# One set of rooms for the moving pieces of attention and feed-forward, filled across the change between them

## The chip, the cores and the metric

The kernel runs on one core of a Trainium2 chip, as one launch. The metric is the device time of the launch in microseconds (us). The kernel before was timed three times: 3040.87, 3048.89 and 3052.48 us, median 3048.89 us. The execution of the profile took 3045.82 us; the span of its trace, from the first to the last instruction, is 3044.1 us. A change of 0.5% is about 15 us.

## What is computed

One inference step of one decoder layer, in float32, for a prompt of 2048 new rows and, with the same weights, for 8 samples of 4 new rows each (32 rows). The model width is 1024.

```python
def decoder_layer(x, s_gla, s_ssm, conv_buf, mk, mv, lw):
    m, s_gla, s_ssm, conv_buf = mixer(rmsnorm(x, lw['ln_mix_pre']), s_gla, s_ssm, conv_buf, lw)
    h = x + rmsnorm(m, lw['ln_mix_post'])
    a = cross_attend(rmsnorm(h, lw['ln_xa_pre']), mk, mv, lw['w_xq'], lw['w_xo'])
    h = h + rmsnorm(a, lw['ln_xa_post'])
    hf = rmsnorm(h, lw['ln_ffn_pre'])
    f = (jax.nn.silu(hf @ lw['w_gate']) * (hf @ lw['w_up'])) @ lw['w_down']
    h = h + rmsnorm(f, lw['ln_ffn_post'])
    return h, s_gla, s_ssm, conv_buf
```

`mixer` is one product with `w_in`, then gated linear attention (GLA) and a state-space part (SSD) with a causal convolution over four rows (`full[:, j:j + t] * lw['ssd_conv_w'][j]`), and a product with `w_out`. For the samples the mixer starts from given states (`state_gla`, `state_ssm`, `state_conv`), and cross attention reads a cache of keys and values for each sample. `w_gate` and `w_up` are 1024 x 2816, `w_down` is 2816 x 1024.

## The kernel before, in words

**Products.** TensorE (PE) multiplies in a reduced float32 form. To keep float32 precision each operand is split into a high part, written by ScalarE (ACT), and a low part, the rest, written by VectorE (DVE); each product is three matmuls (lines 127 to 129). The large products of the second part of the program use in addition a scheme of Strassen's kind: two 2 x 2 block matrices are multiplied with seven products of blocks instead of eight. One operand is *stationary* (loaded into PE as weights) and is made for each unit of work, in tiles named `s`, from an input tile `raw` and sums of it (class `Unit`: the high part in line 1502, the low part in line 1504, the sums in line 1484). The other operand is *moving* and is kept for a whole pass: seven **pieces**, each with a high and a low part, kept in seven **rooms** (tiles `r0` to `r6`).

**Passes.** The second part of the program, from about 918 us on, is a row of passes: "o" (mixer output projection), "s" (attention scores), "v" (attention values), each of 8 units of 256 prompt rows; then three feed-forward passes "g" (gate and up; of 22 units each, over blocks of 768, 768 and 512 prompt rows, the last with the samples); then four passes "d" (down). A unit is seven **groups** of matmuls, one group for each product of blocks, in the order `TURN = [0, 1, 3, 2, 5, 4, 6]`. A group is 12 matmuls, with 512 moving columns in "o", "s" and "v" and 384 in the first two "g" passes. The last group of a unit stands behind the first group of the next one; at the change from "v" to "g" it stands ahead of it. Groups accumulate into PSUM tiles `accA` (two of them), `accB` and `accC`, which ACT and DVE evacuate.

**Filling the rooms.** Class `Pieces` loads each piece in two halves from DRAM into a staging tile `st` (three buffers, which the post-processing also uses) by a DMA of the SP queue; `larger` writes the high part (ACT, line 1566), `smaller` writes the low part (DVE, line 1570) and then loads a later half. For "v" and "g" a half is 512 KB, or 256 KB for the smaller half of a "g" piece. A piece may go into a room when the piece that is in it has had its last matmul. In general the loop over groups makes one half after each group of the last unit of a pass and after each group of the first unit of the next one. The change from "v" to "g" is an exception: rooms of "o", "s" and "v" have `RW = 2048` columns for the high and for the low part, those of "g" have 1536, and `change_rooms` closes the one pool (`rx`) and opens the other (`rf`). So no half is made in the last "v" unit. Behind its last group `change_rooms` is called and two halves are made, and from there on two halves are made after each group of the first "g" unit. For this pass two halves are loaded ahead, for the others three.

**Order of issue.** The groups, the pieces, the evacuations and the post-processing (`posts`: generators, one step after each group; for "v" they are residual, norm, transposes on PE in line 1686, and the writing of the seven feed-forward operands `xp` to DRAM from the POOL queue) are issued in the order in which the loop calls them, and `pin` fixes that order on each engine. Two more queues of generators are stepped at the rates in `RATES` (tenths of a step per group): `aux` (sums of weight blocks) and `back` (the samples' whole layer up to the feed-forward). Steps of `back` are not pinned; a scheduler places their instructions near the group in which they are made. `back` starts in the first "g" pass, when the last of the posts of "v" is done.

**The samples' mixer** (`sample_mixer`) is the first generator of `back`. In one step it makes masks (`rsel`, `rmk` on POOL in lines 931 to 935; `blk`, `bm`, `rst` and others on DVE), loads the convolution rows `cvo`, convolves (lines 984 and 986: 8 and 24 DVE instructions) and applies SiLU; `sample_ssd` and `sample_gla` follow in small steps. In each of them a loop over the 8 samples loads a state, updates it and stores it (for SSD lines 1097 to 1107: two buffers `Ms`, multiplied on POOL in line 1104, added on DVE in line 1105, stored from the POOL queue).

## Time and profile before

| what | value |
|---|---|
| median of the three runs | 3048.89 us |
| profiled execution, its own time | 3045.82 us |
| its span | 3044.1 us |
| PE busy | 2884.3 us (95% of the span) |
| DVE busy | 2087.5 us (69%) |
| ACT busy | 1525.7 us (50%) |
| POOL busy | 544.3 us (18%) |
| mean granted clock of PE | 0.977 |

The time inside the device beside the span is 1.7 us. PE is busy nearly everywhere, so the places where it is not are what can be saved: the profile shows for each instruction how long its engine was idle before it and what ended that idle time ("[2.56 <-ACT r L1566]": 2.56 us, ended by the ACT instruction of line 1566 that wrote `r`). "Busy" of PE counts a matmul as long as it lasts, so a lower clock shows as longer matmuls and not as idle time; the column PEclk, the clock that was granted, has to be read beside it. The change from "v" to "g" lies at about 1469 us.

### The profile page before, as it was taken

How to read it: one execution, taken by the hardware profiler on the slowest of the kernel's cores; microseconds unless marked ns; L12 is line 12 of the kernel's file. 1: busy time of each engine (PE TensorE's matmuls, PEld its weight loads, DVE VectorE, ACT ScalarE, POOL GpSimd, SP SyncE). 2: the span in 40 equal slices, each digit the busy share in tenths (PEclk: the TensorE clock that was granted, in tenths of full speed). 3: DMA queues.
4: the chain of work that ended last, by engine and by line, in shares of the span. 5: the costliest groups of instructions: out<-in, count | busy, mean ns of one | idle time of the engine just before them, and what ended most of it. 6: DMA issues, size and time to landing. Idle time of an engine off the chain costs nothing.

```text
span 3044.1 us, 42288 instructions
## 1 busy us (share of the span) xinstructions
PE 2884.3 (95%) x15207; PEld 2408.6 (79%) x15207; DVE 2087.5 (69%) x3915; ACT 1525.7 (50%) x3044; POOL 544.3 (18%) x749
## 2 busy tenths in 40 slices
PE   8999999999997999999689999999999998999997
PEld 8887777787775778877588888888999995587875
DVE  7666676666737677677587777776678884566576
ACT  4454443554445677776554434433455553444453
POOL 2142341121321321024222100010000000011122
PEclk9999999999999999999799999999999999999998
DMA  7345543242256676467646455774243345767788
GB/s 239 118 152 161 169 125 118 70 128 75 78 187 226 242 263 227 153 202 237 195 177 212 163 172 186 258 265 160 101 150 121 119 141 183 245 139 192 158 210 246
DMA packets 154769, 529.89 MB, mean 174 GB/s; under 512 B 19360, under 2 KB 22608, under 8 KB 143040
## 3 DMA queue, kind: packets, MB, share of 16 engines
q1 hardware_dynamic: 93168, 331.75, 34.1%
q0 software_dynamic: 49152, 170.46, 18.4%
q10 hardware_dynamic: 12240, 24.99, 2.5%
q8 instruction: 120, 1.97, 0.3%
q14 instruction: 89, 0.73, 0.1%
HBM read 373.04 MB, written 154.09 MB: 173 GB/s over the span
## 4 chain that ended last, share of the span: by engine, by line
PE 57%; issue 16%; DMA 7%; DVE 6%; ACT 5%; POOL 2%; POOLq 0%; DVEq 0%; ACTq 0%; SPq 0%
PE accA L127 7%; PE accA L128 7%; PE accA L129 7%; PE accC L127 4%; PE acc L127 4%; PE acc L128 4%; PE acc L129 4%; PE accC L128 4%; PE accC L129 4%; PE accB L127 2%; PE accB L128 2%; PE accB L129 2%; PE mx L1911 1%; PE mx L1686 1%; DMA st<-wT 1%
## 5 line engine op out<-in xcount | busy, mean ns | idle before, releaser
L127 PE MATMUL accA<-r,s 128*128 128x512 f32 (+2 forms) x1792 | 645.3, 360 | 39.0 <-ACT r L1566 13.4
L129 PE MATMUL accA<-r,s 128*128 128x512 f32 (+2 forms) x1792 | 633.6, 354 | 7.1 <-DVE s L1504 6.2
L128 PE MATMUL accA<-r,s 128*128 128x512 f32 (+2 forms) x1792 | 633.9, 354 | 6.7 <-DVE r L1570 6.6
L127 PEld LDWEIGHTS accA<-r,s 128*128 128x128 f32 x1792 | 341.7, 191 | 114.7 <-ACT r L1566 17.5
L1502 ACT ACTIVATE s<-sum 128x512 fp32r<-128x512 f32 (+2 forms) x488 | 289.3, 593 | 268.4 <-DVE sum L1484 102.7
L128 PEld LDWEIGHTS accA<-r,s 128*128 128x128 f32 x1792 | 342.3, 191 | 40.8 <-DVE r L1570 12.0
L129 PEld LDWEIGHTS accA<-r,s 128*128 128x128 f32 x1792 | 341.9, 191 | 38.7 <-DVE s L1504 9.0
L127 PE MATMUL accC<-r,s 128*128 128x512 f32 (+2 forms) x896 | 325.3, 363 | 17.1 <-ACT r L1566 6.8
L1504 DVE TENSOR_TENSOR s<-sum,s 128x512 fp32r<-128x512 f32 (+2 forms) x488 | 308.8, 641 | 35.2 <-ACT s L1502 31.9
L129 PE MATMUL accC<-r,s 128*128 128x512 f32 (+2 forms) x896 | 317.9, 355 | 7.0 <-DVE s L1504 7.0
L128 PE MATMUL accC<-r,s 128*128 128x512 f32 (+2 forms) x896 | 317.6, 354 | 1.0 <-DVE r L1570 0.9
L1504 DVE TENSOR_TENSOR s<-raw,s 128x512 fp32r<-128x512 f32 (+2 forms) x366 | 234.3, 640 | 59.1 <-ACT s L1502 57.6
L1502 ACT ACTIVATE s<-raw 128x512 fp32r<-128x512 f32 (+2 forms) x366 | 218.2, 596 | 54.1 <-PE accC L129 51.3
L121 ACT ACTIVATE whi<-wraw 128x1024 fp32r<-128x1024 f32 (+2 forms) x148 | 137.1, 941 | 211.3 <-PE acc L128 107.2
L127 PEld LDWEIGHTS accC<-r,s 128*128 128x128 f32 x896 | 172.0, 192 | 61.4 <-issue 10.2
L122 DVE TENSOR_TENSOR wlo<-wraw,whi 128x1024 fp32r<-128x1024 f32 (+2 forms) x148 | 166.8, 1136 | 63.4 <-ACT whi L121 62.7
L129 PEld LDWEIGHTS accC<-r,s 128*128 128x128 f32 x896 | 171.8, 192 | 24.7 <-DVE s L1504 8.7
L1570 DVE TENSOR_TENSOR r<-st,r 128x1024 fp32r<-128x1024 f32 (+2 forms) x133 | 136.5, 1028 | 75.1 <-ACT r L1566 74.5
L128 PEld LDWEIGHTS accC<-r,s 128*128 128x128 f32 x896 | 172.0, 192 | 17.1 <-DVE r L1570 2.4
L127 PE MATMUL acc<-xh,whi 128*128 128x512 f32 (+1 forms) x464 | 170.1, 368 | 8.4 <-ACT xh L282 8.2
L129 PE MATMUL acc<-xh,wlo 128*128 128x512 f32 (+1 forms) x464 | 165.3, 358 | 1.7 <-DVE wlo L122 1.7
L128 PE MATMUL acc<-xl,whi 128*128 128x512 f32 (+1 forms) x464 | 164.7, 356 | 0.2 <-DVE xl L283 0.2
(643 smaller groups left out, 5765.0 us busy)
## 6 DMA issues: line engine op xcount, KB each, us to landing
raw<-in_w_gu_dram SPq DMA_DIRECT2D x66, 1024.0 KB, 4.9
wraw<-in_w_in_fm_dram SPq DMA_DIRECT2D x52, 512.0 KB, 3.7
wraw<-in_w_in_tm_dram SPq DMA_DIRECT2D x48, 512.0 KB, 3.7
yp<-y POOLq DMA_DIRECT2D x48, 512.0 KB, 6.9
raw<-aT SPq DMA_DIRECT2D x24, 768.0 KB, 5.3
st<-in_w_down_dram SPq DMA_DIRECT2D x34, 512.0 KB, 6.8
aT<-og POOLq DMA_DIRECT2D x22, 768.0 KB, 4.3
hX<-y POOLq DMA_DIRECT2D x32, 512.0 KB, 5.1
```

The source lines that it names most:

```text
L121: last[0] = nc.scalar.activation(hi[:, cs], raw[:, cs], AF.Copy)
L122: nc.vector.tensor_tensor(lo[:, cs], raw[:, cs], f(hi)[:, cs], op=ALU.subtract)
L127: nc.tensor.matmul(ps, lhsT=wh, rhs=ah, start=start, stop=False, skip_group_check=more)
L128: nc.tensor.matmul(ps, lhsT=wh, rhs=al, start=False, stop=False, skip_group_check=more)
L129: nc.tensor.matmul(ps, lhsT=wl, rhs=ah, start=False, stop=stop, skip_group_check=more)
L1502: nc.scalar.activation(h3, v, AF.Copy)
L1504: return lambda: nc.vector.tensor_tensor(l3, v, f(h3), op=ALU.subtract)
L1570: nc.vector.tensor_tensor(lo, v, f(hi), op=ALU.subtract)
L1686: nc.tensor.transpose(ps[kt // 4][:, kt % 4 * P:(kt % 4 + 1) * P], u[:, kt * P:(kt + 1) * P], ident)
L1911: nc.tensor.matmul(ps[g0:g0 + 32], lhsT=s_f[:, kt].rearrange("p h t -> p (h t)"), rhs=ws.popleft(), start=kt < 4, stop=kt >= FT - 4, tile_ ...
```

## The change

There is one pool of seven rooms, `rp`, with 1536 columns for the high and for the low part, for the whole second part of the program. A piece of "o", "s" or "v" needs 2048 columns for each; it takes the 3072 columns of its room and a further tile of 1024 columns, `e`, in a pool `rx` that is closed when the first "g" pass begins (its space then goes to the pool `pg`). `wide` marks such pieces; the high part and half of the low part lie in the room, the other half of the low part in `e`. `change_rooms` is gone, and with it the exceptions in the loop: halves of the first "g" pass are made as at every other change of pass, one after each group of the last unit of "v" and one after each group of the first unit of "g". Two halves are still loaded ahead for it.

In the samples' mixer the load of `cvo` is issued with the first masks, and the one step becomes ten: three steps pass between the masks of POOL and those of DVE, the other masks and the load's use are in steps of their own, and the convolution is cut after every second of its eight parts. One step ahead of `sample_ssd` is gone. The rate of `back` in the "g" passes goes from 5 to 6 tenths of a step per group.

```diff
@@ sample_mixer
         rmkt = rmk.rearrange("p r s t -> p r (s t)")
+        cvo = mt_([P, 8, NR, 3], "cvo")
+        nc.gpsimd.dma_start(out=cvo, in_=a["state_conv"])
+        yield
+        yield
+        yield
         blk = mt_([NS, NS], "blk")
...
         nc.vector.memset(rst.rearrange("p (r t) -> p r t", t=4)[:, :, 0:1], 0.0)
+        yield
         rsel3 = mt_([96, NR], "rsel3")
...
-        cvo = mt_([P, 8, NR, 3], "cvo")
-        nc.gpsimd.dma_start(out=cvo, in_=a["state_conv"])
+        yield
         nc.vector.tensor_copy(s_xbc[:, :, :, 0:3], cvo)
...
                 nc.vector.scalar_tensor_tensor(c4, s_xbc[:, i, :, j:j + 4], convw[:, i, j:j + 1], c4, op0=ALU.mult, op1=ALU.add)
+            if i % 2:
+                yield
         sxc = cvs
         silu(s_z, s_g, sxc)
+        yield
...
-        yield
         yield from sample_ssd()
@@ pools
-    rp = rctx.enter_context(tc.tile_pool(name="rx", bufs=1, reuse_waits="tile"))
+    rp = ctx.enter_context(tc.tile_pool(name="rp", bufs=1, reuse_waits="tile"))
+    rx = rctx.enter_context(tc.tile_pool(name="rx", bufs=1, reuse_waits="tile"))
...
-    RW = 2048
+    RW = 1536
@@ Pieces.larger
                 r = (ring[1] if k == 7 else rp).tile([P, 2 * RW], F32R, name=f"r{k}")
-                self.at[i] = r[:, 0:RW], r[:, RW:2 * RW]
+                if self.wide:
+                    e = rx.tile([P, 1024], F32R, name=f"e{k}")
+                    self.at[i] = [r[:, c * 1024:(c + 1) * 1024] for c in range(2)], [r[:, 2048:3072], e]
+                else:
+                    self.at[i] = r[:, 0:RW], r[:, RW:2 * RW]
@@ Pieces.moving
+            if self.wide:
+                return [r[k // 2][:, k % 2 * 512:(k % 2 + 1) * 512] for r in self.at[i]]
             return [r[:, k * self.w:(k + 1) * self.w] for r in self.at[i]]
@@ rates and rooms
-    RATES = {"o": (0, 9), "s": (0, 9), "v": (0, 0), "g": (5, 4), "d": (0, 8)}
+    RATES = {"o": (0, 9), "s": (0, 9), "v": (0, 0), "g": (6, 4), "d": (0, 8)}
...
             if i == 0:
+                rctx.close()
                 pg = fctx.enter_context(tc.tile_pool(name="pg", bufs=1, reuse_waits="tile"))
...
-    def change_rooms():
-        nonlocal rp, RW
-        rctx.close()
-        RW = 1536
-        made[0] = 0
-        inside.clear()
-        rp = ctx.enter_context(tc.tile_pool(name="rf", bufs=1, reuse_waits="tile"))
@@ the loop over groups
-        if i == 6 and n + 1 < len(work) and begins[n + 1] and k + 1 == XG:
-            change_rooms()
-            for _ in range(2):
-                coming.step()
...
         p = coming if work[cur][2] == 1 else now if begins[cur] else None
-        if p and p is coming and work[cur][0] + 1 == XG:
-            p = None
         if p:
             p.larger()
         tick()
         if p:
             p.smaller()
-            if p.k == XG:
-                p.step()
```

In the rows below, line numbers of the changed kernel are 5 to 16 higher than those of the kernel before.

**DVE at the change from "v" to "g".** Rows of DVE's order in the kernel before, from the last groups of "v" (line 1673 adds a PSUM tile to `y`) to the second group of "g" (line 1794 evacuates gate values); line 1570 is the low part of a half of a piece, 1504 that of a stationary operand:

```order
L1673 TENSOR_TENSOR y<-accA,y 128x512
L1504 TENSOR_TENSOR s<-raw,s 128x512
L1484 TENSOR_TENSOR sum<-sum,raw 128x512
L1695 TENSOR_TENSOR u<-mx,cols 128x512
L1570 TENSOR_TENSOR r_13309<-st,r_13309 128x4x256
L1570 TENSOR_TENSOR r_13309<-st,r_13309 128x4x128
L1504 TENSOR_TENSOR s<-sum,s 128x512
```

The same stretch of the changed kernel, begun four groups earlier (1689 is the line 1673 of before, 1584 the line 1570, 1513 the line 1504, 1493 the line 1484):

```order
L1669 SCALAR_TENSOR_TENSOR y<-y,rs,ga 128x1024
L1584 TENSOR_TENSOR r_13268<-st,r_13268 128x4x256
L1689 TENSOR_TENSOR y<-accC,y 128x512
L1513 TENSOR_TENSOR s<-raw,s 128x512
L1493 TENSOR_TENSOR sum<-raw 128x512
L1584 TENSOR_TENSOR r_13268<-st,r_13268 128x4x128
L1689 TENSOR_TENSOR y<-accA,y 128x512
L1513 TENSOR_TENSOR s<-raw,s 128x512
L1493 TENSOR_TENSOR sum<-sum,raw 128x512
L1711 TENSOR_TENSOR u<-mx,cols 128x512
L1584 TENSOR_TENSOR r_13329<-st,r_13329 128x4x256
L1513 TENSOR_TENSOR s<-sum,s 128x512
```

Before, the first low part of a "g" piece (`r_13309`) stands behind the last of "v"; now the third and fourth piece (`r_13268`, `r_13329`) are being made there, one half per group, in between the work of "v".

**SP's queue at the same place.** Before (line 1617 loads a half of a "g" piece, 1516 the input of a "g" unit):

```order
L1617 DMA st<-xp 128x2x512
L1617 DMA st<-xp 128x512
L1516 DMA raw<-in_w_gu_dram 128x2048 x2
L1617 DMA st<-xp 128x2x512
L1617 DMA st<-xp 128x512
L1617 DMA st<-xp 128x2x512
```

and now (1633 and 1525 are the same lines):

```order
L1633 DMA st<-xp 128x2x512
L1633 DMA st<-xp 128x512
L1525 DMA raw<-in_w_gu_dram 128x2048
L1633 DMA st<-xp 128x2x512
L1633 DMA st<-xp 128x512
L1633 DMA st<-xp 128x2x512
L1633 DMA st<-xp 128x512
L1525 DMA raw<-in_w_gu_dram 128x2048
L1633 DMA st<-xp 128x2x512
```

Four loads of halves have moved ahead of the input of the second "g" unit.

**DVE in the samples' convolution.** Before (984 and 986 are the convolution, 1794 an evacuation, 1504 the stationary operand that PE needs next):

```order
L1794 TENSOR_TENSOR sg<-accC,sg 128x384
L977 COPY s_xbc<-cvo 128x64x3
L1504 TENSOR_TENSOR s<-raw,s 128x512
L979 COPY cvo<-s_xbc 128x192
L984 TENSOR_SCALAR cvs<-s_xbc,cols 128x32 x2
L986 SCALAR_TENSOR_TENSOR cvs<-s_xbc,cols,cvs 128x32 x6
L984 TENSOR_SCALAR cvs<-s_xbc,cols 128x32 x2
L986 SCALAR_TENSOR_TENSOR cvs<-s_xbc,cols,cvs 128x32 x6
L984 TENSOR_SCALAR cvs<-s_xbc,cols 128x32 x2
L986 SCALAR_TENSOR_TENSOR cvs<-s_xbc,cols,cvs 128x32 x6
```

and now, of its first two parts (989 and 991 are the convolution):

```order
L989 TENSOR_SCALAR cvs<-s_xbc,cols 128x32
L1493 TENSOR_TENSOR sum<-raw,sum 128x512
L1513 TENSOR_TENSOR s<-sum,s 128x512
L991 SCALAR_TENSOR_TENSOR cvs<-s_xbc,cols,cvs 128x32
L1493 TENSOR_TENSOR sum<-raw 128x512
L1414 TENSOR_TENSOR st<-st 128x512
L991 SCALAR_TENSOR_TENSOR cvs<-s_xbc,cols,cvs 128x32
L1415 TENSOR_TENSOR st<-st 128x512
```

The convolution no longer stands as one block of 32 instructions between two stationary operands.

8 lines of the change are left out of this document (4 added, 4 removed).

## The prediction

> **What bounds the kernel now.** I read the page first: busy times, slices, granted clock.
>
> ```profile
> PE 2884.3 (95%) x15207; PEld 2408.6 (79%) x15207; DVE 2087.5 (69%) x3915; ACT 1525.7 (50%) x3044; POOL 544.3 (18%) x749
> PE   8999999999997999999689999999999998999997
> PEclk9999999999999999999799999999999999999998
> ```
>
> PE is busy for 95% of the span, so a change that takes no matmul away can only win where PE waits or its clock is lowered. In one slice of 40 both happen: the twentieth (1446 to 1522 us), with PE at 6 tenths and the clock at 7. That is the change from "v" to "g". I cut the trace there into stages, with ordinary stages and the two other changes of pass of attention beside them.
>
> ```profile
> core 0: us, PE busy (x) PEld busy (x) DVE busy (x) ACT busy (x) POOL busy (x), PEclk, DMA share, GB/s
> 1443.53:1468.96 25.43, 24.26 (x115) 19.43 (x113) 17.96 (x34) 18.83 (x47) 10.50 (x16) 1.00 0.85 260
> 1468.96:1521.97 53.01, 30.26 (x101) 25.41 (x101) 27.31 (x44) 24.54 (x48) 10.05 (x15) 0.65 0.56 170
> 1521.97:1543.24 21.27, 18.64 (x100) 17.85 (x101) 14.54 (x28) 12.46 (x29) 6.74 (x11) 0.92 0.44 164
> 1443.53:1543.24 99.71, 73.16 (x315) 62.69 (x314) 59.80 (x104) 55.83 (x122) 27.29 (x42) 0.79 0.61 192
> 1543.24:1585.12 41.88, 34.75 (x191) 32.19 (x191) 36.94 (x121) 20.94 (x39) 8.70 (x16) 0.92 0.48 172
> 1602.40:1636.70 34.30, 34.30 (x195) 30.01 (x195) 24.26 (x45) 12.76 (x24) 6.73 (x9) 1.00 0.63 209
> 2169.00:2227.00 58.00, 58.00 (x336) 58.00 (x336) 38.65 (x65) 25.56 (x48) 1.52 (x2) 1.00 0.28 97
> 1095.50:1146.00 50.50, 43.87 (x201) 35.74 (x200) 43.37 (x64) 42.04 (x76) 10.63 (x17) 0.97 0.81 281
> 1277.50:1319.40 41.90, 39.88 (x189) 32.39 (x188) 37.28 (x55) 37.92 (x82) 1.60 (x3) 1.00 0.70 245
> ```
>
> The first three rows are the last eight groups of "v" and the first two units (14 groups) of "g"; the fourth row is their sum. 2169 to 2227 us is "g" undisturbed: 336 matmuls, 28 groups, so 2.07 us for a group. The first "g" unit takes 53.01 us where seven groups cost 14.5. What PE waits for there:
>
> ```profile
> 1475.07 0.69 PE L127 MATMUL accB<-r,s 128*128 128x384 f32 x1 [2.56 <-ACT r L1566]
> 1478.95 0.69 PE L128 MATMUL accB<-r,s 128*128 128x384 f32 x1 [3.19 <-DVE r L1570]
> 1487.07 0.69 PE L127 MATMUL accC<-r,s 128*128 128x384 f32 x1 [4.23 <-ACT r L1566]
> 1513.13 0.69 PE L127 MATMUL accA<-r,s 128*128 128x384 f32 x1 [4.23 <-ACT r L1566]
> ```
>
> Each group waits for its own piece. Why the piece comes late shows on ACT and DVE, one group long:
>
> ```profile
> 1482.88 0.56 DVE L1794 TENSOR_TENSOR sg<-accB,sg 128x384 f32<-128x384 f32 x1 [3.98 <-PE accB L129]
> 1483.47 0.52 ACT L1795 ACTIVATE sg<-sg 128x384 f32<-128x384 f32 x1 [7.15 <-DVE sg L1794]
> 1484.42 1.04 ACT L1566 ACTIVATE r<-st 128x1024 fp32r<-128x1024 f32 x1
> 1485.49 1.23 DVE L1570 TENSOR_TENSOR r<-st,r 128x1024 fp32r<-128x1024 f32 x1 [1.20 <-ACT r L1566]
> 1486.40 0.61 ACT L1566 ACTIVATE r<-st 128x512 fp32r<-128x512 f32 x1
> 1487.05 0.69 DVE L1570 TENSOR_TENSOR r<-st,r 128x512 fp32r<-128x512 f32 x1 [0.33 <-ACT r L1566]
> ```
>
> ACT and DVE are idle for 4 to 7 us and then everything runs in a row: group ends, evacuation, SiLU, first half, second half, next group (1482.88 to 1487.07). No engine is full: it is one chain, with PE's clock at 0.65 on top.
>
> **The change, part by part.**
>
> *Pieces filled across the change.* No instruction disappears; 14 halves on ACT and DVE and their loads move ahead, by eight groups the first and by less the later ones. Afterwards each piece is finished one group or more before PE wants it, so the chain is cut; what is left is the work. For the stretch of 99.71 us, work is: PE 25.43 for the groups of "v" as they are, plus 14 x 2.07 = 29.0, plus four batches of transposes at 1.09 us (row of line 1686 below), together 58.8; DVE 59.80; ACT 55.83; DMA 0.61 x 99.71 = 60.8. So four resources lie at 56 to 61 us, and none of the moved work is free: its cover is only each other. The floor is 61 us. How near a change of pass comes to its floor, the last two rows tell: 50.50 us for 43.37 of DVE (1.16 times) and 41.90 for 37.92 of ACT (1.10), PE's own work being no larger than that floor by much. I take 1.12: 68 us, a gain of 31.7. Bounds: 1.0 (61 us, gain 38.7) and 1.2 (73 us, gain 26.7). What is late next is the post-processing of "v", whose transposes stand in PE's order and wait for ACT:
>
> ```profile
> 1531.40 1.09 PE L1686 MATMUL mx<-ident,u 128*128 128x128 f32 x8 [2.34 <-ACT u L1725]
> ```
>
> The moved DMAs go past others. SP now issues four of them ahead of the input `raw` of the second "g" unit, and the next stands behind it; queued behind a load that waits for a staging tile are therefore a `raw` and the later halves, and ACT, in order, stops at the half that has not landed, with the evacuations behind it. Times to landing around the change, the first two rows in the last unit of "v":
>
> ```profile
> raw<-in_w_gu_dram SPq DMA_DIRECT2D x1, 1024.0 KB, 6.0
> st<-xp SPq DMA_DIRECT2D x1, 512.0 KB, 10.3
> st<-xp SPq DMA_DIRECT2D x6, 512.0 KB, 6.3
> st<-xp SPq DMA_DIRECT2D x6, 256.0 KB, 3.6
> ```
>
> Two halves are ahead, that is two groups of "v", about 6.3 us (25.43 / 8 x 2): about the 6.3 us of the median and less than 10.3. This is inside the factor 1.12 if it happens once or twice, and a rival if it happens at each. The Trainium skill ("DMA: Bandwidth & Descriptors", section "Issuing engines are not separate DMA queues") says that DMAs issued by SP, ACT and GpSimd run on the same 16 DMA engines and interleave; that speaks against moving loads under the writes of "v" on POOL's queue. The row of 10.3 us at a DMA share of 0.85 agrees with it, and if it held for every half the outcome would be the first rival's.
>
> The rooms' new shape costs nothing that I can see: the same matmuls, casts and subtractions with the same sizes, only other addresses. If it cost one per cent of the groups of attention it would be 5 us; nothing in the trace speaks for that, and I keep it out of the sum.
>
> *Samples' masks and convolution in steps.* In the kernel before PE stands still a second time, in the third "g" unit:
>
> ```profile
> 1565.71 0.66 PE L127 MATMUL accA<-r,s 128*128 128x384 f32 x1 [6.31 <-DVE sps L155]
> 1553.79 0.17 DVE L938 COPY blk<-rsel 32x32 f32<-32x32 f32 x1 [1.97 <-POOL rsel L932]
> L986 DVE SCALAR_TENSOR_TENSOR cvs<-s_xbc,cols,cvs 128x32 f32<-128x32 f32 x24 | 4.2, 233 | 0.0
> L984 DVE TENSOR_SCALAR cvs<-s_xbc,cols 128x32 f32<-128x32 f32 x8 | 2.0, 283 | 0.0
> ```
>
> The named releaser is a tiny operation; the cause is the 1.97 us in which DVE waits for POOL's mask and the 6.2 us of convolution, all in front of the stationary operands that PE needs. In steps, the mask is ready before DVE comes to it, and the convolution is cut to pieces of about 1.5 us, which DVE's lead over PE covers (in 1602 to 1636 us DVE is busy 24.26 of 34.30 with the samples running, and PE waits for nothing); without that cover it would cost the 6.2 us again. These two units (1543.24 to 1585.12) took 41.88 us; the two quiet ones with samples took 34.30, the groups alone 29.0. So the gain lies between 7.6 and, with 1 us of the samples' own matmuls, 11.9. I take 9. The nine added steps hold no instruction.
>
> *The rate, 6 instead of 5.* PE's work for the samples is the same, in fewer groups. Where a step is limited by its own chain of load, POOL, DVE and store, fewer groups hide it. That is so in the loop that updates the SSD states:
>
> ```profile
> 1643.53 0.28 PE L1102 MATMUL mx<-sxw,sBm 96*128 96x256 f32 x1
> 1685.50 0.36 PE L1102 MATMUL mx<-sxw,sBm 96*128 96x256 f32 x1 [2.09 <-DVE sBm L1099]
> 1666.15 1.04 POOL L1104 TENSOR_TENSOR Ms<-Ms,sell 128x512 f32<-128x512 f32 x1 [7.10 <-DMA Ms<-in_state_ssm_dram]
> 1667.22 0.69 DVE L1105 TENSOR_TENSOR Ms<-Ms,mx 128x512 f32<-128x512 f32 x1 [6.49 <-POOL Ms L1104]
> 1668.56 0.44 PE L129 MATMUL accA<-r,s 128*128 128x384 f32 x1 [3.13 <-DVE s L1504]
> ```
>
> First and last of eight samples: 41.97 us, 6.0 for a step, where two groups are 4.14 us. DVE waits in order for POOL, POOL for the state's DMA, PE for DVE. With 1.67 groups to a step the chain stays at 6.0 and PE has 0.33 x 2.07 = 0.7 us less to do in it: 7 x 0.7 = 5 us lost. Lower bound -3 (the samples leave the second "g" pass earlier, where they share DMA with its change of pass), upper 12 (the same loss in the GLA state loop and a few of the cache loads). I take +5.
>
> **Sum.** Against the profiled execution, 3045.82 us: -31.7 - 9 + 5 = 3010.1. The median of the runs stands 3.07 higher (3048.89), so I predict 3013 us. The bounds together: -38.7 - 11.9 - 3 gives 2995, -26.7 - 7.6 + 12 gives 3027.
>
> **The rivals.** *Loads set the pace of the pieces* (0.20). If a load can start only when the half two before it has been used, a piece costs 6.3 + 1.04 + 1.23 us and about 0.5 for issue and semaphores, 9 us; six pieces after the first, begun at about 1450 us, are ready at 1504 instead of about 1522, and the gain at the change is 18 instead of 32: 3027 us, and with 10.3 us in the "v" unit 3035. For it: only two halves ahead, DMA already at 0.85. Against: there are three staging tiles, and the post-processing holds one only for part of the time.
>
> *Everything overlaps* (0.20). The stretch reaches its floor, the samples give 11 and the rate costs nothing: 3045.8 - 38.7 - 11 + 3.1 = 2999. For it: in the undisturbed stages PE is at 100% with DVE at two thirds. Against: at no change of pass so far.
>
> *The samples' loads become the bound* (0.05, slower). The samples have some 88 steps that each load a state, a weight or a cache block. If each kept the time it has now instead of shrinking with the groups, as the SSD loop does, PE would lose 0.7 us in each: 61 us, against 41 gained, so 3069 us. It decides from the point where a step's load takes longer than 1.67 groups and its matmuls. Against it: apart from the SSD loop PE waits for hardly anything there (the row 1602 to 1636: 34.30 busy of 34.30).
>
> *The halves only move the wait* (0.05): made in the last "v" unit they delay its own stationary operands on ACT and DVE, as much as the first "g" unit gains. All but some 5 of the 31.7 is lost, the samples' 9 and the rate's 5 remain: 3045.8 - 5 - 9 + 5 + 3.1 = 3040, no change that a measurement of this kernel can tell from none (0.5%, 15 us).
>
> **How the numbers follow.** The likeliest case has 0.50, with its own range 2995 to 3027. The overlap case lies at its lower end, the load case at and beyond its upper end. To leave no more than 2 in 10 outside I take 2998 to 3034. Faster by over 0.5% means below 3033.6: all of the likeliest and of the overlap case, and most of the load case (0.17 of 0.20), 0.87; within 0.5%: the rest of it and the moved wait, 0.08; slower: 0.05.
>
> **What would show it.** Right: no row of PE with "<-ACT r" or "<-DVE r" above 1 us in the first "g" unit, that unit at 17 to 22 us with the granted clock above 0.9, the last eight groups of "v" at 26 to 30 us, the ACT rows of the pieces waiting on PE or DVE and hardly on "DMA st<-xp"; no PE wait above 2 us in the third "g" unit; the SSD loop at 6 us for a step again, with more PE idle time. Wrong: ACT rows of the pieces with waits of 3 us and more on "DMA st<-xp" (loads); a last "v" unit beyond 35 us (moved wait); PE waits on `sraw`, `Ms` or `Gs` all through 1600 to 2100 us (samples' loads).

## The result, and the profile after

The changed kernel takes 3022.76 us (median of four runs, 3019.78 to 3024.43), the kernel before, timed beside it, 3049.85 us (3040.87 to 3052.48). The ratio is 0.9915, 95% interval 0.9893 to 0.9938: faster by 0.85%, and by more than 0.5% over the whole interval. The forecast was 3013 us with the range 2998 to 3034: the sign and the range held, the gain came out as 27 us where 36 had been forecast.

The page of the changed kernel, the rows that answer to the first three of the prediction (busy time of PE, its slices, the granted clock in slices):

```profile
PE 2879.0 (95%) x15207; PEld 2404.9 (80%) x15207; DVE 2088.2 (69%) x3915; ACT 1523.0 (50%) x3043; POOL 541.6 (18%) x749
PE   8999999999998899999899999999999999999997
PEclk9999999999998999999999999999999999999998
```

The slice with PE at 6 tenths and the clock at 7 is gone. The same stages in the view by windows: the last eight groups of "v", the first "g" unit, the second, the sum of the three, then the third and fourth "g" unit, and behind these everything up to the second unit of the third "g" pass (42 units, with the samples in them):

```profile
core 0: us, PE busy (x) PEld busy (x) DVE busy (x) ACT busy (x) POOL busy (x), PEclk, DMA share, GB/s
1446.04:1478.01 31.97, 26.81 (x115) 21.81 (x114) 23.63 (x41) 22.57 (x51) 11.60 (x16) 0.89 0.88 275
1478.01:1503.87 25.86, 18.97 (x101) 18.01 (x100) 21.36 (x38) 20.20 (x41) 9.71 (x15) 0.87 0.85 258
1503.87:1523.27 19.40, 16.98 (x102) 16.14 (x102) 14.05 (x28) 12.89 (x31) 7.06 (x12) 1.00 0.52 189
1446.04:1523.27 77.23, 62.76 (x316) 55.96 (x315) 59.04 (x104) 55.66 (x122) 28.37 (x42) 0.91 0.78 248
1523.27:1554.33 31.06, 29.55 (x170) 28.97 (x169) 29.07 (x74) 12.35 (x24) 8.72 (x16) 1.00 0.61 217
1554.33:2274.21 719.88, 703.73 (x4114) 633.48 (x4114) 518.92 (x966) 317.69 (x596) 63.75 (x98) 0.99 0.53 182
```

Beside the rows of before: 99.71 us became 77.23, 41.88 became 31.06. For the last stage the kernel before has 716.33:

```profile
1585.12:2301.45 716.33, 699.44 (x4094) 631.38 (x4092) 512.94 (x918) 311.09 (x582) 67.83 (x98) 0.99 0.54 183
```

Of the 22.5 us at the change from "v" to "g", 10.4 are busy time of PE (73.16 less 62.76: the same matmuls, at a mean clock of 0.91 instead of 0.79) and 12.1 are idle time (26.55 less 14.47). Where that rest of 14.47 lies, the view by tile says for the transposes of the post-processing, and the timeline row by row:

```profile
L1702 PE MATMUL mx<-ident,u x51: 272/273/474, 1445.8 to 1519.0; 128*128 128x128 f32 x51
  ACT u L1741: 14.3, 5
1460.88 1.97 PE L1702 MATMUL mx<-ident,u 128*128 128x128 f32 x8 [3.71 <-ACT u L1741]
1474.34 1.09 PE L1702 MATMUL mx<-ident,u 128*128 128x128 f32 x8 [1.46 <-ACT u L1741]
1489.89 1.97 PE L1702 MATMUL mx<-ident,u 128*128 128x128 f32 x8 [5.45 <-ACT u L1741]
1500.85 1.09 PE L1702 MATMUL mx<-ident,u 128*128 128x128 f32 x8 [1.35 <-ACT u L1741]
1512.81 1.09 PE L1702 MATMUL mx<-ident,u 128*128 128x128 f32 x8 [2.37 <-ACT u L1741]
```

No matmul waits for a piece any more. 14.3 us, in five waits, are for ACT's `u`, the operand of the transposes. The pieces themselves, with what their engines were idle for ahead of them (us, times), and their loads (KB, median us to landing):

```profile
L1580 ACT ACTIVATE r<-st x14: 612/835/1061, 1450.1 to 1502.7; 128x1024 fp32r<-128x1024 f32 x7, 128x512 fp32r<-128x512 f32 x7
L1584 DVE TENSOR_TENSOR r<-st,r x14: 684/956/1227, 1451.2 to 1503.3; 128x1024 fp32r<-128x1024 f32 x7, 128x512 fp32r<-128x512 f32 x7
  ACT r L1580: 9.2, 8
  DVE r L1584: 0.6, 2
st<-xp SPq DMA_DIRECT2D x6, 512.0 KB, 4.9
st<-xp SPq DMA_DIRECT2D x6, 256.0 KB, 4.7
```

All 14 halves are made between 1450 and 1504 us. DVE waits for ACT ahead of eight of them, and two weight loads wait for DVE, 0.6 us together. The loads are hardly waited for, but with little to spare: the slowest, issued at 1465.6 us, took 10.1 us to land, just as ACT came to its half at 1475.77, and the last landed 0.1 us too late.

### The profile page after: what moved, and what is told of

It is laid out like the page before. It is cut to its first block, busy times and chain, and to the rows that moved or that the text cites. A ratio compares the mean times of both kernels' runs of the same rounds, so it can differ in the third digit from the quotient of the medians.

```text
span 3022.3 us, 42283 instructions
## 1 busy us (share of the span) xinstructions
PE 2879.0 (95%) x15207; PEld 2404.9 (80%) x15207; DVE 2088.2 (69%) x3915; ACT 1523.0 (50%) x3043; POOL 541.6 (18%) x749
## 4 chain that ended last, share of the span: by engine, by line
PE 55%; issue 17%; DVE 7%; DMA 7%; ACT 5%; POOL 2%; POOLq 0%; DVEq 0%; ACTq 0%; SPq 0%
PE accA L127 7%; PE accA L128 6%; PE accA L129 6%; PE acc L127 4%; PE acc L128 4%; PE acc L129 4%; PE accC L127 3%; PE accC L128 3%; PE accC L129 3%; PE accB L127 2%; PE accB L128 2%; PE accB L129 2%; PE mx L1927 1%; PE mx L1702 1%; DVE s L1513 1%
## 5 line engine op out<-in xcount | busy, mean ns | idle before, releaser
L127 PE MATMUL accA<-r,s 128*128 128x512 f32 (+2 forms) x1792 | 645.1, 360 | 26.4 <-DVE y L1891 5.7
L129 PE MATMUL accA<-r,s 128*128 128x512 f32 (+2 forms) x1792 | 632.3, 353 | 3.2 <-DVE s L1513 3.1
L128 PE MATMUL accA<-r,s 128*128 128x384 f32 (+2 forms) x1600 | 556.4, 348 | 1.7 <-DVE r L1584 1.5
L127 PEld LDWEIGHTS accA<-r,s 128*128 128x128 f32 x1792 | 341.9, 191 | 101.3 <-issue 23.4
L129 PEld LDWEIGHTS accA<-r,s 128*128 128x128 f32 x1792 | 341.6, 191 | 35.4 <-DVE s L1513 4.4
L127 PE MATMUL accC<-r,s 128*128 128x512 f32 (+2 forms) x896 | 324.4, 362 | 14.8 <-ACT y L1889 4.3
L128 PEld LDWEIGHTS accA<-r,s 128*128 128x128 f32 x1600 | 305.2, 191 | 26.2 <-DVE r L1584 4.0
L129 PE MATMUL accC<-r,s 128*128 128x512 f32 (+2 forms) x896 | 318.2, 355 | 7.6 <-DVE s L1513 7.6
L128 PE MATMUL accC<-r,s 128*128 128x384 f32 (+2 forms) x800 | 279.1, 349 | 0.0
L127 PEld LDWEIGHTS accC<-r,s 128*128 128x128 f32 x896 | 171.1, 191 | 56.7 <-ACT y L1889 10.2
L129 PEld LDWEIGHTS accC<-r,s 128*128 128x128 f32 x896 | 171.7, 192 | 25.8 <-DVE s L1513 9.2
L135 POOL TENSOR_TENSOR rs<-ms,nhalf 128x1 f32<-128x1 f32 (+4 forms) x125 | 104.2, 836 | 324.3 <-DVE ms L133 317.2
L128 PEld LDWEIGHTS accC<-r,s 128*128 128x128 f32 x800 | 153.1, 191 | 11.2 <-issue 0.8
```

The costliest lines, as they stand in the source:

```text
L127: nc.tensor.matmul(ps, lhsT=wh, rhs=ah, start=start, stop=False, skip_group_check=more)
L128: nc.tensor.matmul(ps, lhsT=wh, rhs=al, start=False, stop=False, skip_group_check=more)
L129: nc.tensor.matmul(ps, lhsT=wl, rhs=ah, start=False, stop=stop, skip_group_check=more)
L135: nc.gpsimd.tensor_tensor(out=rs[:rows, :cols], in0=ms[:rows, :cols], in1=nhalf[:rows, :cols], op=ALU.pow)
```

## The stages of all runs

Every kernel below was traced once, so what differs between two executions of one kernel cannot be told apart here from what differs between two kernels. This table cuts each span at the same places in PE's order (starts of groups): the start of the second part, passes "o" and "s", "v" up to its last eight groups, the change up to the third "g" unit, the third and fourth "g" unit, the 42 units behind them, units 3 to 20 of the third "g" pass, and the rest. Us.

| kernel | up to | "o", "s" | "v" | change | g 3, 4 | next 42 | third "g" | rest | span |
|---|---|---|---|---|---|---|---|---|---|
| before | 918.0 | 374.8 | 150.7 | 99.7 | 41.9 | 716.3 | 193.4 | 549.2 | 3044.1 |
| changed | 916.3 | 378.4 | 151.3 | 77.2 | 31.1 | 719.9 | 193.8 | 554.2 | 3022.3 |
| rooms alone | 915.5 | 374.9 | 151.0 | 78.0 | 41.4 | 717.4 | 193.5 | 548.7 | 3020.3 |
| steps alone | 917.2 | 377.8 | 151.2 | 97.6 | 31.1 | 717.3 | 193.5 | 551.2 | 3036.9 |
| rate 5 | 913.9 | 376.7 | 151.3 | 79.8 | 30.7 | 717.2 | 193.4 | 549.2 | 3012.3 |
| rate 4 | 916.7 | 376.4 | 150.8 | 77.8 | 30.9 | 724.8 | 193.8 | 550.6 | 3021.9 |
| halves behind | 915.1 | 373.8 | 151.3 | 81.5 | 30.8 | 723.0 | 193.5 | 552.0 | 3021.0 |
| no DVE half | 917.5 | 378.4 | 150.8 | 71.3 | 31.1 | 721.2 | 193.5 | 548.0 | 3011.8 |
| transposes later | 919.5 | 372.3 | 143.8 | 75.5 | 31.2 | 713.2 | 193.5 | 549.1 | 2998.0 |
| rate 4.5 | 914.9 | 374.7 | 151.3 | 77.1 | 31.4 | 713.0 | 193.5 | 552.1 | 3008.0 |
| later, 4.5 | 916.5 | 374.1 | 143.8 | 74.3 | 34.5 | 719.4 | 193.5 | 549.2 | 3005.4 |
| later, 4.5, "o" too | 914.5 | 367.7 | 144.0 | 74.6 | 35.9 | 720.7 | 193.5 | 552.2 | 3003.0 |
| masks only | 915.4 | 370.5 | 150.9 | 77.3 | 33.1 | 720.8 | 193.8 | 549.4 | 3011.2 |
| DVE alone | 917.9 | 376.8 | 151.5 | 69.2 | 30.8 | 721.9 | 193.5 | 551.4 | 3013.1 |

The expectations below speak of a window that begins two matmuls later: what is 77.2 us in this table is 76.7 us there.

Two columns repeat within 1 us wherever their part of the program is the same, "v" and the third "g"; the change repeats within 3 us. "o", "s" and the rest do not: in kernels whose code there is the same they lie between 370.5 and 378.4 and between 548.0 and 554.2. The changed kernel's traced execution is at the upper end in both. For "o" and "s" the windows show where the spread comes from; here are the kernel before, the changed kernel and "masks only":

```profile
918.02:1292.79 374.77, 347.96 (x1584) 281.87 (x1585) 275.57 (x447) 257.17 (x555) 68.15 (x109) 0.97 0.64 221
916.30:1294.71 378.41, 352.48 (x1585) 284.92 (x1585) 275.76 (x447) 257.35 (x555) 68.27 (x109) 0.95 0.63 219
915.37:1285.87 370.50, 344.67 (x1585) 279.02 (x1585) 275.65 (x447) 257.00 (x555) 68.10 (x109) 0.98 0.65 224
```

PE is idle for 26.8, 25.9 and 25.8 us; what differs is its busy time, by 7.8 us between the last two, at a granted clock of 0.95 and 0.98. This spread is the same matmuls at another mean clock, and not more waiting.

## The experiments

**The parts apart.** The rooms and the early filling alone; `sample_mixer` and the rate as before:

```diff
 (of the change, only pools, Pieces and the loop over groups)
-    RATES = {... "g": (6, 4), ...}
+    RATES = {... "g": (5, 4), ...}
     sample_mixer: as in the kernel before
```

> The rooms and the early filling alone; the samples' masks and convolution as in the kernel before, the rate 5. Theory (each edit pays in its own stage): the last eight groups of v and the first two units of g take 77 us in the place of 99.7, a gain of 23; the third and fourth g units keep their stall of about 6 us, 41 to 42 us for the two; no other stage moves, so the profiled execution is 23 us shorter than the one before: about 3023 us, between 3018 and 3028. Rival (the samples' stall came from the late change of pass, and goes with it): the third and fourth g units take 31 to 33 us here too, and the kernel comes to about 3013. On the two losses that nobody forecast (about 3 us in the o pass, 5 us in the d pass of the changed kernel): if they come from the new shape of the rooms they are in this run too, if they are the spread between executions they are not, or not both.

Measured: 3024.41 us, ratio 0.9948 (0.9929 to 0.9966), against 3042.6 us of the kernel before on the same chip. In the trace:

```profile
1441.33:1519.31 77.98, 62.84 (x316) 56.01 (x314) 59.09 (x104) 55.64 (x122) 28.89 (x42) 0.91 0.76 245
1541.56 0.66 PE L127 MATMUL accA<-r,s 128*128 128x384 f32 x1 [6.32 <-DVE sps L155]
```

21.7 us at the change, and the wait of the samples stays to a hundredth (6.32 against 6.31): the two places are independent, the rival falls. "o", "s" and the rest are as in the kernel before (374.9 and 548.7 us), so in this trace the rooms' shape brings neither of the two losses that nobody had forecast.

The other half, the samples' steps alone, in the rooms of before:

```diff
     sample_mixer: as in the change
     everything else, and the rate 5: as in the kernel before
```

> The samples' masks and convolution in steps alone; rooms, filling and rate 5 as in the kernel before. Theory (each edit pays in its own stage): the change from v to g takes 99 to 100 us again, the third and fourth g units take 31 to 33 us in the place of 41.9, a gain of 9 to 11: 3035 to 3037 us for the profiled execution against 3045.8. Rival (the stall went with the earlier change of pass): the two units keep 39 to 42 us, and the time stays within 3 us of the kernel before. If the losses in the o and the d pass belong to the new rooms, neither is here.

Measured: 3031.28 us, ratio 0.9964 (0.9951 to 0.9977).

```profile
1446.27:1543.87 97.60, 71.99 (x315) 61.81 (x314) 59.89 (x104) 55.84 (x122) 27.31 (x42) 0.81 0.61 196
1543.87:1574.97 31.10, 29.53 (x170) 28.95 (x169) 29.07 (x74) 12.34 (x24) 8.72 (x16) 1.00 0.60 214
```

10.8 us at the place itself; the 42 units behind it take 1.0 us more (717.3 against 716.3; why stays open): 9.8 us net. The span says 7.2 us, since "o", "s" and the rest were longer here by 5.0 and the other stages shorter by 2.4.

**The rate.** 5 and 4 instead of 6, on the changed kernel:

```diff
-    RATES = {... "g": (6, 4), ...}
+    RATES = {... "g": (5, 4), ...}      # and (4, 4)
```

> The changed kernel with the rate back at 5. Theory (the loop over the SSD states is bound by its own chain of load, POOL, DVE and store, about 6 us a step, so fewer groups to hide it cost PE time): units 29 to 62 take 5 us less than in the changed kernel; 3017 to 3018 us for the profiled execution against 3022.8 of the changed kernel's median. Rival (the samples' steps cost PE the same at any rate, and the 5 us were the spread of one execution): no difference, 3021 to 3024. Second rival (a slower rate holds the samples' traffic into the second g pass and its change): 2 us slower than the changed kernel.

> The changed kernel with the rate at 4, so 2.5 groups to a step of the samples. Theory (chain-bound loops): 2.5 groups are 5.2 us, still under the 6 us of a step in the SSD loop, so PE gains 0.5 group in each of its seven steps and something in the GLA loop: 5 to 9 us less than with 5 if nothing is left over; but 34 units at rate 5 become 42.5, which ends at unit 66 or 67, where whatever is left is issued at once before the third g pass: 0 to 10 us of it back. About 3013, between 3008 and 3022. Rival (the rate costs nothing): the same time as the changed kernel plus the leftover at the end, 3023 to 3033.

Measured: 3012.64 us with 5, ratio 0.9902 (0.9886 to 0.9919), and 3022.99 us with 4, ratio 0.9935 (0.9919 to 0.9951). The 42 units behind the change at 5, and the last 8 of them at 4 and at 6; then the loop over the SSD states at 6, 5 and 4 (first and last start of 16 matmuls, two for each of the eight samples):

```profile
1552.47:2269.62 717.15, 699.06 (x4114) 631.48 (x4114) 520.52 (x966) 316.43 (x596) 67.43 (x98) 0.99 0.53 183
```

```profile
2128.23:2277.45 149.22, 132.38 (x788) 117.33 (x787) 96.84 (x173) 61.39 (x122) 9.48 (x14) 0.93 0.47 159
```

```profile
2158.10:2274.21 116.11, 112.54 (x674) 111.53 (x673) 84.66 (x144) 57.73 (x110) 3.06 (x4) 0.97 0.38 133
L1110 PE MATMUL mx<-sxw,sBm x16: 277/281/357, 1636.5 to 1667.8; 96*128 96x256 f32 x16
```

```profile
L1110 PE MATMUL mx<-sxw,sBm x16: 277/281/384, 1654.9 to 1687.3; 96*128 96x256 f32 x16
```

```profile
L1110 PE MATMUL mx<-sxw,sBm x16: 277/281/384, 1679.7 to 1718.0; 96*128 96x256 f32 x16
```

From 6 to 5 the 42 units gain 2.7 us, about half of the 5 expected, and from 5 to 4 they lose 7.7, because 33 us of leftover (149.22 against 116.11) are issued at once ahead of the third "g" pass; I had expected at most 10. A step of the SSD loop takes about 4.5 us at 6, 4.6 at 5 and 5.5 at 4 (31.3, 32.4 and 38.3 us over seven), where the groups to a step are 3.45, 4.14 and 5.18. So the loop is held back, by 1.0, 0.5 and 0.3 us a step, but not by a chain of 6.0 us.

**Why the change from "v" to "g" keeps 77.2 us.** First the order on ACT: the half of a piece behind the step of post-processing.

```diff
-        if p:
+        if p and p.k != XG:
             p.larger()
         tick()
+        if p and p.k == XG:
+            p.larger()
         if p:
             p.smaller()
```

> The changed kernel with ACT's half of each piece of the first g pass issued behind the group's step of post-processing instead of ahead of it; nothing else. In the changed kernel the last eight groups of v and the first two g units take 76.7 us, and 14.3 us of that are five waits of transposes for ACT's u (3.7, 1.5, 5.4, 1.3, 2.4). Theory H (the halves stand in front of u on ACT): four of the five have a half of 0.6 or 1.04 us directly ahead of u, 3.3 us together, and with DVE behind it somewhat more; the stretch takes 71 to 74 us. Rival D (DVE and the round trips from engine to engine are what is late): the waits stay at 13 us and more, the stretch at 75 to 79. Rival L (now the pieces are late): new waits of PE for r, the stretch above 79 us.

Measured: 3026.6 us, ratio 0.9936 (0.9917 to 0.9954); the stretch takes 81.5 us. Of the 4.2 us more, 3.0 are busy time of PE (65.79 against 62.76, at a clock of 0.87 instead of 0.91).

```profile
1485.94 1.97 PE L1702 MATMUL mx<-ident,u 128*128 128x128 f32 x8 [6.46 <-ACT u L1741]
1496.76 1.09 PE L1702 MATMUL mx<-ident,u 128*128 128x128 f32 x8 [0.47 <-ACT u L1741]
1502.06 0.57 PE L127 MATMUL accA<-r,s 128*128 128x384 f32 x1 [2.12 <-ACT r L1580]
```

The small waits shrink (1.35 to 0.47 us), the longest grows (5.45 to 6.46), and PE waits 2.1 us for a piece: theory H falls, and what was seen is rival L (pieces late, a stretch longer than 79 us). Then less work, first for DVE (the low parts of the pieces of the first "g" pass are not made, the high parts are used in their place), then for ACT (DVE rounds by a copy, ACT makes nothing of these pieces):

```diff
-                nc.vector.tensor_tensor(lo, v, f(hi), op=ALU.subtract)
+                if not skip:          # skip: pieces of the first "g" pass
+                    nc.vector.tensor_tensor(lo, v, f(hi), op=ALU.subtract)
...                           # and Pieces.moving gives the high part for both
```

> The changed kernel with DVE's half of the pieces of the first g pass left out (the low parts are not made, and the high ones are used in their place, so the products of this pass are those of rounded pieces): 14 instructions, 13.5 us of DVE, go from the stretch of 76.7 us; every matmul stays. Theory D (what is late is DVE, which stands at 58.5 us of 76.7): the waits of the transposes shrink from 14.3 to under 7 us and the stretch to 68 to 71 us. Theory H (ACT's halves ahead of u): the stretch stays at 74 us or more. A third reading (the chain of post-processing itself, its trip to the memory and back and POOL's rs): no change, 76 to 78 us.

```diff
-            nc.scalar.activation(hi, v, AF.Copy)
+            if not skip:
+                nc.scalar.activation(hi, v, AF.Copy)
...
+                if skip:
+                    nc.vector.tensor_copy(hi, v)
...                           # else the subtraction; Pieces.moving as above
```

> The changed kernel with ACT's half of the pieces of the first g pass left out: DVE rounds them by a copy in the place of the subtraction, and the high parts stand for the low ones too, as in the run without DVE's half. So ACT loses 14 instructions and 11.6 us, and DVE keeps 14 of about the same size. Theory E (neither engine alone is the bound; each trip through PE, ACT and DVE counts, so taking either one's work away gives about half of it): the stretch takes 69 to 73 us of 76.7. Rival D (DVE alone is late): 75 to 78 us, where the run without DVE's half took 70.8. Rival A (ACT is the worse one): under 69 us.

Measured, each timed once: 3013.59 and 3014.75 us. First the run without DVE's half, then the one without ACT's; in each the last eight groups of "v" and then the whole stretch:

```profile
1446.74:1473.13 26.39, 24.09 (x116) 19.60 (x114) 18.81 (x35) 20.58 (x46) 10.89 (x16) 1.00 0.93 308
1446.74:1518.00 71.26, 59.61 (x315) 53.85 (x314) 47.32 (x90) 55.53 (x122) 27.17 (x42) 0.95 0.81 268
```

```profile
1446.21:1471.65 25.44, 24.09 (x116) 19.63 (x114) 20.12 (x39) 17.29 (x44) 11.29 (x16) 1.00 0.93 305
1446.21:1515.46 69.25, 59.47 (x315) 53.72 (x314) 53.30 (x104) 45.55 (x108) 28.29 (x42) 0.95 0.84 276
```

Taking 11.7 us from DVE (59.04 to 47.32) shortens the stretch by 6.0; taking 10.1 us from ACT and 5.7 from DVE (its copies took less time than its subtractions) shortens it by 8.0. If DVE alone were late, the second edit should have gained less than the first; it gained more, so ACT counts too. How much is ACT's the runs do not say, since the second edit takes work from both (with 68.7 us in the window of the expectations it lies just under theory E's range, and in rival A's). Neither edit reaches the floor of 61 us. About half of what is removed comes out as time, but not as waiting alone: the waits of the transposes fall from 14.3 us only to 11.6 and 9.7 (theory D had under 7), and 3.2 and 3.3 us are PE's busy time, at a clock of 0.95 instead of 0.91. The last eight groups of "v" cost 26.39 and 25.44 us, hardly more than before the change (25.43), where both operations make them 31.97. One wait goes with neither, the one of 5.45 us: it is 6.20 and 6.09 us in these two runs. Its rows in the changed kernel, on DVE, ACT and POOL:

```profile
1484.07 0.15 DVE L1664 TENSOR_TENSOR sq<-ss 128x1 f32<-128x1 f32 x1
1486.65 0.55 DVE L1810 TENSOR_TENSOR sg<-accB,sg 128x384 f32<-128x384 f32 x1
1485.59 1.58 POOL L135 TENSOR_TENSOR rs<-ms,nhalf 128x1 f32<-128x1 f32 x1
1487.24 0.52 ACT L1811 ACTIVATE sg<-sg 128x384 f32<-128x384 f32 x1 [2.27 <-DVE sg L1810]
1488.71 1.13 ACT L1741 ACTIVATE u<-y,rs 128x1024 f32<-128x1024 f32 x1
```

DVE works without a pause from 1478 to 1488 us, among other things on the sums of two blocks of rows (lines 1414 to 1418, 2.8 us), and the gate's evacuation (1486.65) and the square root's input (1484.07) stand behind them; ACT idles 2.27 us for that evacuation and has `u` at 1489.84. This is the post-processing of "v" meeting the first gate of "g". That the pieces are not its cause is shown by the two runs, in which it stays; which of the other links makes it was not tested.

So the transposes were given one group more of distance:

```diff
         u = yield from after_rows(j, m, y, ss, "ln_xa_post", None)
+        yield
         turned(u, gff)
```

> The changed kernel with the transposes of v's post-processing one group later in the order (all through the pass; the rest of the step unchanged). Theory: PE waits because it comes to the transposes one group after ACT's u is issued, and ACT and DVE run behind by 1.3 to 5.4 us there; one group is 2.07 to 2.72 us, so the waits of 3.7, 1.5, 5.4, 1.3 and 2.4 us shrink to about 1, 0, 3, 0, 0, a gain of 8 to 10 us if the lag stays: 67 to 70 us for the stretch of 76.7. Rival (the lag is work, not distance: ACT and DVE need their 55 to 58 us with the idle time of round trips between, and PE waits elsewhere instead, for evacuations or stationary operands): the stretch keeps 74 to 78 us.

Measured: 3000.88 us, ratio 0.9852 (0.9835 to 0.9869). The stretch takes 75.5 us: the rival was right there. What PE waits for instead, the two longest waits:

```profile
1462.70 0.79 PE L127 MATMUL accA<-r,s 128*128 128x512 f32 x1 [5.66 <-DVE y L1689]
1486.41 0.69 PE L127 MATMUL accA<-r,s 128*128 128x384 f32 x1 [3.47 <-ACT r L1580]
```

One group waits for DVE's evacuation, one for a piece. The gain lies elsewhere and I had not forecast it: in the undisturbed units of "v" PE waited for `u` at every transpose, 0.4 us, and a unit took 22.1 us; with the distance it takes 20.85, and the stage "v" 7.6 us less. That and the change (1.8) make 9.4 us. The 24.3 us by which this traced execution is shorter than the changed kernel's are more than that: 5.1 are the rest and 6.1 "o" and "s", whose code is the same; 6.7 are the 42 units, of which below; and the second part began 3.2 later. In "o" and "s" PE is busy 345.93 us here, at a clock of 0.98, and 352.48 in the changed kernel, at 0.95. I count these stages as spread between executions, but that is not shown: the four timed executions of this kernel all lie between 2998.9 and 3003.0 us, those of the changed kernel between 3019.8 and 3024.4.

**More of the rate.** 4.5 on the changed kernel, then with the later transposes, then with the transposes of the "o" pass later too:

```diff
+    RATES = {... "g": (4.5, 4), ...}
```

> The changed kernel with the rate at 4.5, between the two that were measured: units 28 to 69 took 719.8 us at 6, 717.1 at 5, and at 4 the units 28 to 57 took 23 to 30 us less than at the others, with 31 us of leftover in front of the third g pass. Theory (chain-bound steps; the leftover was what the rate was too slow for): the samples' steps end near unit 64, before they are issued at once in front of the third pass; units 28 to 69 take 708 to 714 us, so 3006 to 3013 us for the execution. Rival (the samples cost PE the same sum at any rate, only elsewhere): 716 to 720, no faster than with 5.

> The transposes of v's post-processing one group later, and the rate 4.5, both on the changed kernel. Theory (the two act in different stages, the one in the v pass, 7.7 us, and at the change, 1.6 us; the other in units 28 to 69, 6.8 us): the sum, 3005 to 3009 us for the profiled execution if the start and the d pass are like those of the changed kernel's, 2991 to 2996 if they are like those of the run with the later transposes alone (3000.9 median); against that run 5 to 8 us faster. Rival (part of the 20 us that the later transposes gained was the spread of executions, or the rate's gain goes when the samples start earlier): within 3 us of 3000.9.

> As the run before, and in the o pass too the transposes one group later. Theory (in the undisturbed units of the o pass PE waits for ACT's u at each transpose as it did in v, 22.0 us a unit where 20.85 are its groups): units 4 to 6 take 20.9 us, and the o pass, eight units, 8 to 12 us less. Rival (the o pass is held by DVE and ACT, which do the sums for the next weights there: the wait goes elsewhere): less than 3 us. Second rival (the input of the s pass is written one group later and its first units wait for it): s begins 2 to 4 us worse.

Measured: 3008.88 us, ratio 0.9885 (0.9860 to 0.9909); 3009.04, ratio 0.9877 (0.9858 to 0.9897); 2998.7, ratio 0.9843 (0.9823 to 0.9862). At 4.5 the 42 units take 713.0 us on the changed kernel, as theory said. With the later transposes and the same rate they take 719.4, and with the later transposes and the rate 6 they take 713.2. So the two gains do not add: the second kernel is 8 us slower than the later transposes alone, where the theory had 5 to 8 us faster and the rival the same. Its third and fourth "g" unit are longer too (34.5 us against 31.2). The 42 units at 4.5, on the changed kernel and with the later transposes:

```profile
1549.37:2262.39 713.02, 698.28 (x4113) 630.81 (x4114) 524.29 (x966) 316.06 (x596) 65.33 (x98) 0.99 0.54 184
```

```profile
1543.31:2262.70 719.39, 703.72 (x4115) 633.74 (x4114) 520.72 (x964) 315.65 (x594) 65.45 (x98) 0.99 0.54 182
```

So the rate between 4.5 and 6 does not set this stage by itself: at 6 it was 719.9 to 723.0 in five kernels and 713.2 in the sixth, at 4.5 713.0, 719.4 and 720.7, at 5 716.3 to 717.4 in four. Of the 6.4 us between the two rows, 5.4 are busy time of PE. In the traces' record of the granted clock, it stands at half for 10.2 us of the first row and 20.5 us of the second, so up to 5 us of the difference are the clock. How the samples' steps fall against the groups may decide this; the rule behind it stays open. In the third kernel the "o" pass takes 7.4 us less than in the second, of which the "s" pass takes back 0.9: somewhat less than the 8 to 12 expected. Two of its three undisturbed units went from 22.0 to 20.9 us; the other 5 us are no more than the spread of this pass, 198.9 to 207.7 us in the kernels whose code is the same there. That last kernel and the one with the later transposes alone are the fastest, 1.5% under the kernel before.

**Which of the samples' steps.** The changed kernel without the four steps in the convolution:

```diff
-            if i % 2:
-                yield
```

> The changed kernel without the four steps inside the convolution: the masks' steps and the early load stay. Theory (2 us of waiting for the mask and 6.2 us of convolution, both in front of the operands that PE needs): the convolution stays in one piece, PE waits 3 to 5 us for it again in the third or fourth g unit, and the two units take 35 to 38 us, between 31.1 with all steps and 41.9 without. Rival A (the wait for the mask alone was the cause): 31 to 32 us. Rival B (the convolution alone was): 39 to 42 us.

Measured, timed once: 3012.97 us.

```profile
1514.03:1547.15 33.12, 30.16 (x170) 28.98 (x170) 31.43 (x89) 14.94 (x31) 8.68 (x16) 1.00 0.56 201
1547.15 0.41 PE L127 MATMUL accA<-r,s 128*128 128x384 f32 x1 [1.22 <-DVE sps L154]
```

33.1 us lies between theory (35 to 38) and rival A (31 to 32), near the one in which the masks, the early load and the steps around them do nearly all: 8.8 of the 10.8 us, the cut of the convolution 2.0. The longest wait is 1.2 us and not 3 to 5. These shares rest on one trace, in a stage that takes 30.7 to 35.9 us in kernels with all the steps.

## Why the prediction was right, and where its sum was off

*Pieces filled across the change (-31.7 forecast, -22.5 measured, -21.7 alone).* The mechanism was right: no matmul waits for a piece any more. The loads land in 4.9 and 4.7 us (medians) and cost 0.1 us of waiting, so the case of the pace set by loads fell. It was not far off: the row of 10.3 us came again once, as 10.1 us, on a load that landed just in time, and the last two pieces were ready only as PE came to them, not "one group or more before". The Trainium skill's rule that was cited with it ("DMA: Bandwidth & Descriptors", section "Issuing engines are not separate DMA queues") foretells interleaving. At a DMA share of 0.88 in the last groups of "v" the trace shows next to no price for it: over the stretch the 256 KB halves landed later than before (4.7 us against 3.6), the 512 KB halves sooner (4.9 against 6.3). "What is late next" was right too: the transposes, for ACT's `u`. The gain lies outside the bounds of this term, 26.7 to 38.7 us. What was mis-sized is the factor 1.12 over the floor of 61 us, taken from the two other changes of pass. It is 1.27 here (77.23 / 60.8). The two rows that it came from set the time against DVE and ACT, but PE was busy longer there (43.87 of 50.50 us, 39.88 of 41.90), which makes 1.15 and 1.05; and the floor that it was put on, 61 us, was that of DMA. Two things were seen at this change: the last eight groups of "v" pay 6.5 us as soon as ACT and DVE both make halves in them (31.97 against 25.43; the sign of 26 to 30 us failed), and the post-processing of "v" meets the first gate in one chain through DVE, POOL and ACT (5.4 us of wait, then 1.3 and 2.4; the sign of 17 to 22 us for the first "g" unit failed at 25.86, and the clock there was 0.87 instead of above 0.9). The sum also took PE's 58.8 us at the full clock, where its busy time was 62.76. The rival "the halves only move the wait" was thus right by 6.5 us, in the last unit of "v", where it had put 26.7.

*Samples' steps (-9 forecast, -10.8 at the place, -9.8 alone with what follows).* Right, with the sign: the longest wait in the third "g" unit is 1.45 us. The shares were not told; the one run with the convolution in one piece gives the masks and the steps around them four fifths.

*The rate (+5 forecast, +3.6 in the trace of the change, +2.7 against rate 5).* Inside the bounds of -3 and 12, but the step that was to explain it failed: a step of the SSD loop is not a chain of 6.0 us. At the rate of 6 it takes 4.5; the 6.0 of the kernel before held four waits of PE, 7.3 us together (two of them in the rows that the prediction shows), and without them it would have been 5.0. And the extra time of the 42 units shows as busy time of PE (703.73 against 699.06 us at rate 5) and not as more idle time, as I had written. The clock is a part of that: it stood at half for 13.7 us of these units, against 10.2 at rate 5, which makes under 2 of the 4.7 us. The rest was not settled. The sign of the price holds in most orders, not in all (713.2 us once at 6), so that the sum came within 1.4 us of it is in part luck.

*The rest.* The sum had nothing for the parts that the change does not touch, and the traced execution has 9.7 us there (3.6 in "o" and "s", 5.0 in the rest, 1.0 in "v" and the third "g"), less 1.7 up to the start. In "o" and "s" PE is busy 4.5 us longer at a lower clock and idle 0.9 us less. The view by windows of the rest, before and after:

```profile
2494.89:3044.10 549.21, 511.35 (x2106) 376.95 (x2104) 331.59 (x610) 236.77 (x483) 74.85 (x103) 0.97 0.74 197
2468.05:3022.30 554.25, 511.81 (x2106) 377.85 (x2104) 331.89 (x610) 236.84 (x483) 74.90 (x103) 0.97 0.73 196
```

Here PE works as long as before; 4.6 of the 5.0 us are waiting (37.9 against 42.4 us, and 42.5 in the run of the steps alone, with the old rooms). In the other traces, of old and of new rooms, the same parts spread over 370.5 to 378.4 and 548.0 to 552.2 us. So neither loss is shown to belong to the change; nor is it excluded for the 2 us by which the rest lies above that spread. By the stages it does touch, the change is worth 22.5 + 10.8 - 3.6 = 29.7 us; the forecast for them was 35.7, and the 6.0 between are the first term (9.2 too much) less the two others (1.8 and 1.4 too cautious).

## What to carry to other kernels

When a stall between two passes is removed by starting the next one's preparation earlier, what the busiest engine has to do there is a floor that need not be reached: here the stretch stayed at 1.27 times that floor, and two edits that took 11.7 and 15.8 us of work from DVE and ACT gained 6.0 and 8.0 us. That each trip PE, DVE, ACT, PE waits in order behind the work of the engines on its way is the likely reason; it was argued from the rows and not tested apart. After such a change look at the steady units of the neighbouring pass too; a wait of 0.4 us at every transpose, too small to be noticed in the list of waits, was worth 7.6 us in one pass, and giving the consumer one group more of distance removed it. And price each stage from stages, not from whole times: two stages of this kernel differ by 6 and 8 us between traces while others repeat within 1 us. Look at idle time and granted clock apart when you do.

## What the hardware showed that was not expected

A wait of PE can be paid twice, once as idle time and once more as matmuls at a lower clock. The eight transposes of one step take 1.09 us after waits of 1.35 to 2.37 us, and 1.97 us after waits of 3.71 and 5.45 (in the run with the halves behind also after 6.46, and 1.09 after 0.47). At the main place of the change 10.4 of the 22.5 us that were gained were busy time of PE and no idle time at all. The Trainium skill says in "TensorE: Matmul & The Clock Gate", section "What's actually happening", that the clock falls to half after an idle window of about 3.4 us. The five waits of the changed kernel agree with that, but two shorter waits of the kernel before, whose rows the prediction shows, do not. The matmuls ahead of the wait of 2.56 us took 0.33 us, and the one behind it 0.69 us, as long as behind 4.23 us; one behind 0.49 us took 0.44. Behind the wait of 2.34 us the transposes still took 1.09 us, but a moment later the matmuls went from 0.34 to 0.52 us and stayed there for 3.4 us:

```profile
1532.51 0.34 PE L128 MATMUL accA<-r,s 128*128 128x384 f32 x1
1532.90 0.52 PE L127 MATMUL accA<-r,s 128*128 128x384 f32 x1
```

So these traces give no single length from which a wait is paid. In their record of the granted clock it is either full or half, and within a trace all its changes lie on a grid of 3.41 us. Where a wait of 2 to 3 us falls on that grid may decide whether it is paid; this was not tested apart. The prediction counted PE at the full clock behind the change; the waits that were left bring it to 0.91 there.

The spread between traces is uneven. Over the 14 of them units 3 to 20 of the third "g" pass took 193.4 to 193.8 us, and the stage "v" with the same order 150.7 to 151.5, but "o" and "s" with the same code 370.5 to 378.4, and the "d" passes with the end 548.0 to 554.2.
